# Strassen products in the second MLP projection, with weight sums formed by accumulating transfers

## The chip, the core and the metric

The kernel runs on one core of a Trainium2 chip. Its five engines work side by side: TensorE multiplies matrices into PSUM, VectorE and ScalarE do the elementwise work, GpSimd (POOL) here does masks, a few small operations and some transfers, and SyncE (SP) only issues DMAs. They wait for one another on semaphores. The metric is device time in microseconds (us) of one execution.

## The reference

The program is one layer of a decoder: three mixing branches (a gated delta rule, a gated linear recurrence, attention into a memory), a merge, and then an MLP. The change touches only the MLP, which is, with 256 positions, width 2048 and 8192 hidden columns:

```
h2 = rmsnorm(x, g_pre_mlp[l])
m = jnp.square(jax.nn.relu(h2 @ w_mlp_in[l])) @ w_mlp_out[l]
x = x + rmsnorm(m, g_post_mlp[l])
```

All data are fp32. TensorE's rounded form of fp32 keeps fewer bits, so each operand is split into a high part (its rounded copy) and a low part (the rest), and a product of two operands is taken as three matmuls: high x high, high x low, low x high.

## The kernel before, in words

**Slices.** The hidden columns are cut into 8 slices of 1024 (`NE`, index `e`). `mlp_in(e)` makes the hidden values of slice e, and `mlp_out(e)` multiplies them by the slice's 1024 rows of `w_mlp_out` and adds the result to the accumulators `yacc`. The program goes `mlp_in(0)`, then `mlp_in(e)`, `mlp_out(e-1)` for e = 1 to 7, and `mlp_out(7)` at the end.

**First projection.** `mlp_in(e)` has two units of 512 hidden columns (`unit_stacked`). The weights are the stationary operand there, and the moving one is either 512 wide (high and low activations side by side, a wide matmul) or 256 (high only, a narrow one): 64 wide and 64 narrow matmuls a unit, over 8 weight tiles that are taken in pairs, once with the wide matmuls first and once with the narrow ones. At a unit's end ScalarE copies out one half of each of the four PSUM tiles, VectorE adds the other (four `relu` rows of 128x256), squares the positive part (128x1024), and the value is split into `mh` and `ml`.

**Second projection.** `mlp_out(e)` has four chunks c of 512 output columns; each takes 4 weight tiles of two k-tiles of 128 rows (`KG` = 2), for two token tiles t (`NT` = 2) and three products: 4 x 4 x 2 x 2 x 3 = 192 matmuls of 512 columns. The stationary operands are the tokens, the moving ones the weights. After a chunk VectorE adds two PSUM tiles to `yacc` (in the first slice ScalarE copies them there; in the last one the sums go on to the final norm).

**Weights.** A weight tile is 128 partitions x 2 x 512 fp32, 512 KB. SP's queue loads it (`load_w_raw`) into a ring of raw tiles `w`; `split_w` has ScalarE cast it to `wh` and VectorE subtract to make `wl`, each in a ring of four. A slice takes 16 tiles for each projection. A load can start when the split of the tile that had its buffer is done; a split can write when the matmuls on the old pair are done.

**Order.** The framework's scheduler sets one order of instructions for each engine from a cost model ahead of time, and an engine takes its instructions strictly in that order. Some small jobs are generators in a list `bg`, of which a few steps are pumped after each group of matmuls (`tick`). PSUM has two double tiles in the pool `pmm` and four single tiles in the pool `pbp` (`bank`). All operations of VectorE, ScalarE and TensorE are recorded at one line, L56, the helper that issues them, so that a row is known by its tiles.

Of the kernel before, what the change touches and what calls it, by code (L numbers as in the profile page):

```python
# [10 lines left out]
F32 = mybir.dt.float32  # L11
# [29 lines left out]
def tile_trunk(ctx: ExitStack, tc, a):  # L41
# [31 lines left out]
    wp = ctx.enter_context(tc.tile_pool(name="wp", bufs=4))  # L73
    hp = ctx.enter_context(tc.tile_pool(name="hp", bufs=4))
    gp = ctx.enter_context(tc.tile_pool(name="gp", bufs=25))
    lp = ctx.enter_context(tc.tile_pool(name="lp", bufs=1))
# [4 lines left out]
    pbp = ctx.enter_context(tc.tile_pool(name="pbp", bufs=4, space=bass.MemoryType.PSUM))  # L81

# [24 lines left out]


# [14 lines left out]
    def load_grow(names, c0, q):  # L123
        grow = const(f"grow{c0}", [len(names) * 16, P])
# [84 lines left out]
    def unit(act, nk, src, c0, r0=0, order=None, split=False, post=None, ws=None):  # L209

        if split:
            ps = [bank("mm") for _ in range(2)]
        else:
            both = pmm.tile([P, 1024], F32, tag="mm", name=nm("mm"))
            ps = [both[:, 0:512], both[:, 512:1024]]
        if order is None:
            order = [(g, None) for g in range(nk // KG)]  # L220
        ws = ws or {}
        for i, (g, tt) in enumerate(order):
            k0 = g * KG
            if g not in ws:
                ws[g] = load_w(src, r0 + k0, KG, c0)
            wh, wl = ws[g]
            for j in range(KG):
                kt = k0 + j
                ah, al = act(kt)
                for t in range(NT) if tt is None else (tt,):  # L230
                    o = ps[t]
                    st, sl = ah[:, t * P:(t + 1) * P], al[:, t * P:(t + 1) * P]
                    T.matmul(o, st, wh[:, j, :], start=kt == 0, stop=False)
                    T.matmul(o, st, wl[:, j, :], start=False, stop=False)
                    T.matmul(o, sl, wh[:, j, :], start=False, stop=kt == nk - 1)
            tick()
            if post is not None and i + 1 in post:
                post[i + 1](ps)
        return ps if split else both
# [20 lines left out]
    def unit_stacked(pairs, nk, src, c0, ps):  # L260

        for gg in range(0, nk // KG, 2):
            groups = []
            for g in (gg, gg + 1):
                k0 = g * KG
                groups.append((k0, load_w(src, k0, KG, c0),
                               [flat(pairs[kt // 4][:, kt % 4]) for kt in range(k0, k0 + KG)]))
# [164 lines left out]
    mgt, mlt, caus = const("mgt", [P, P]), const("mlt", [P, P]), const("caus", [P, P])  # L432
    mgtr, onesr = const("mgtr", [P, P], F32R), const("onesr", [P, P], F32R)
    msk2 = const("msk2", [P, 2, P])
    dblk = const("dblk", [P, BL])

    mblk = const("mblk", [P, P])
    rfirst, rsecond = const("rfirst", [P, 1]), const("rsecond", [P, 1])
    mT = {s: const(f"mT{s}", [P, P]) for s in (1, 2, 4, 8, 16, 32, 64)}

    def gen_masks():
# [12 lines left out]
        for s in (1, 2, 4, 8, 16, 32, 64):  # L454
            b = 2 * s
            if b < P:
                cur = cst.tile([P, P], F32, tag=f"blk{b.bit_length() % 2}", name=f"blk{b}")
# [8 lines left out]
            d = cst.tile([P, P], F32, tag="mdiff", name=f"mdiff{s}")  # L466
# [23 lines left out]
    rbm = const("rbm", [P, S])  # L490
# [13 lines left out]
    def gen_start():  # L504
# [11 lines left out]
        crow = const("crow", [96, P])  # L516
        adma(crow, a["conv_a"][0].rearrange("t (c p) -> (t c) p", p=P))
        lrow = const("lrow", [8, P])
# [78 lines left out]
    ccol = const("ccol", [P, 96])  # L597
    lbl1, lba = const("lbl1", [P, 8]), const("lba", [P, 8])
    gna, gnb = const("gna", [P, P]), const("gnb", [P, P])
    alog, dtb = const("alog", [P, 8]), const("dtb", [P, 8])  # L600
# [87 lines left out]
    beta = const("beta", [P, NT, 8])  # L688
    ld = const("ld", [P, NT, 8])
    ldh, ldl = const("ldh", [P, NT, 8], F32R), const("ldl", [P, NT, 8], F32R)  # L690
# [613 lines left out]
    gbc = load_gbc(a["g_post_mix"])  # L1304

# [79 lines left out]
    st2 = const("st2", [P, 8])  # L1385

    def gen_s2():
        for c in range(4):
            for t in range(NT):
                j = g4("junk")  # L1390
                A.activation(j[:, 0:512], xs[c][:, t, :], AF.Square, accum_out=st2[:, t * 4 + c:t * 4 + c + 1])
            yield
# [6 lines left out]

    h2act = act_of(h2T)  # L1400
    yacc = [None] * 4
# [3 lines left out]
    first = [(g, t) for t in range(NT) for g in range(4)] + [(g, None) for g in range(4, 8)]  # L1405

    def gen_turn(r, hi, lo):
# [3 lines left out]
        for hh in range(2):  # L1411
            for q in range(2):
                for t in range(NT):
# [3 lines left out]
            split_psum(pt[:, hh * 512:(hh + 1) * 512].rearrange("p (q s) -> p q s", q=2),  # L1417
                       hi[:, hh * 2:hh * 2 + 2, :], lo[:, hh * 2:hh * 2 + 2, :])
            yield

    def mlp_in(e):
        mt = []
        for u in range(2):
            c0 = e * 1024 + u * 512
            hi, lo = g4("mh", (P, 4, S), F32R), g4("ml", (P, 4, S), F32R)
            r = g4("relu")
            if e == 0 and u == 0:
                ps = unit(h2act, KT, a["w_mlp_in"][0], c0, order=first, ws=ahead)
                A.activation(r, ps, AF.Relu)
                V.scalar_tensor_tensor(out=r, in0=ps, scalar=0.0, in1=r, op0=ALU.max, op1=ALU.mult)  # L1430
                bg.append(gen_turn(r, hi, lo))
            else:
# [7 lines left out]
                unit_stacked(h2B, KT, a["w_mlp_in"][0], c0, ps)  # L1440
                r4 = r.rearrange("p (c s) -> p c s", c=4)
                for c in range(4):
                    A.copy(r4[:, c, :], ps[c][:, S:2 * S])
                    V.tensor_tensor(out=r4[:, c, :], in0=ps[c][:, 0:S], in1=r4[:, c, :], op=ALU.add)
                V.scalar_tensor_tensor(out=r, in0=r, scalar=0.0, in1=r, op0=ALU.max, op1=ALU.mult)
                split_psum(r4, hi, lo)
            mt.append((hi, lo))
        return mt

    def mlp_evac(c, t, p_):  # L1450
        y_ = yacc[c][:, t, :]
        V.tensor_tensor(out=y_, in0=p_, in1=y_, op=ALU.add)
        j = g4("junk")
        A.activation(j[:, 0:512], y_, AF.Square, accum_out=stf[:, t * 4 + c:t * 4 + c + 1])
        return y_

    def final(ps, t):
        y3 = mlp_evac(3, t, ps[t])
        yg = g4("yg")[:, 0:512]
        V.tensor_tensor(out=yg, in0=y3, in1=gb(3), op=ALU.mult)  # L1460
# [4 lines left out]
        for c in range(4):  # L1465
            x_, y_ = xs[c][:, t, :], yacc[c][:, t, :] if c < 3 else yg
# [3 lines left out]
    def mlp_out(e, mt):  # L1470
        for c in range(4):
            args = (act_of(mt), 8, a["w_mlp_out"][0], c * 512, e * 8)
            if e == NE - 1 and c == 3:
# [3 lines left out]
                          post={4: lambda ps: final(ps, 0)})  # L1477
                final(ps, 1)
                continue
            ps = unit(*args, split=c >= 2)  # L1480
            if c < 2:
                ps = [ps[:, t * 512:(t + 1) * 512] for t in range(NT)]
            if e == 0:
                yacc[c] = g4("yacc", (P, NT, 512))
            for t in range(NT):
                if e == 0:
                    A.copy(yacc[c][:, t, :], ps[t])
                elif e < NE - 1:
                    V.tensor_tensor(out=yacc[c][:, t, :], in0=ps[t], in1=yacc[c][:, t, :], op=ALU.add)
                else:  # L1490
                    y_ = mlp_evac(c, t, ps[t])
                    V.tensor_tensor(out=y_, in0=y_, in1=gb(c), op=ALU.mult)

    prev = mlp_in(0)
    bg.append(gen_s2())
    for e in range(1, NE):
        cur = mlp_in(e)
        if e == 4:
            gbc = load_gbc(a["g_post_mlp"])
        mlp_out(e - 1, prev)  # L1500
        prev = cur
    drain()
    mlp_out(NE - 1, prev)
# [14 lines left out]
```

## Time and profile before

| | |
|---|---|
| Runs | 1793.5, 1793.82, 1794.29 us, median 1793.82 |
| The profiled execution, first to last instruction | 1792.7 us, mean granted TensorE clock 0.999 |
| Busy: TensorE | 99%, 9137 matmuls |
| VectorE, ScalarE, POOL | 64%, 51%, 3% |
| DMA | 336.60 MB, 188 GB/s on average |
| Weight tiles of `w_mlp_out` | 128 transfers of 512 KB from SP's queue, 3.9 us from issue to landing |

The median of the runs is 1.1 us above the profiled span. In the profile's rows, "busy" is time in which an instruction of an engine was running; the idle time before an instruction is put down to the semaphore that released it. Buffer numbers are left out of names in the profile, and kept in the rows of the order below.

### The profile page before, as it was taken

The numbers are of one execution on the slowest core, as the hardware profiler recorded it, in microseconds if no ns is written. First come the engines' busy times: TensorE is split into PE (matmuls) and PEld (weight loads), VectorE is DVE, ScalarE is ACT, GpSimd is POOL, SyncE is SP. The second block draws the span as 40 slices with busy tenths as digits, with TensorE's granted clock in tenths as the row PEclk, the third lists the DMA queues.
The fourth block names the chain that finished last, engine by engine and source line by source line (L and its number), as shares of the span: only waits on it lengthen the run. The fifth ranks groups of instructions, "written<-read, shape, count | busy, mean of one in ns | idle before, by whom it ended". The sixth has DMA issues, their size and how long they took to land.

```text
span 1792.7 us, 23771 instructions
## 1 busy us (share of the span) xinstructions
PE 1780.9 (99%) x9137; PEld 1517.3 (85%) x9137; DVE 1151.3 (64%) x1599; ACT 905.8 (51%) x1156; POOL 58.6 (3%) x100
## 2 busy tenths in 40 slices
PE   9999999999999999999999999999999999999998
PEld 7888888888888888888888888888888888888886
DVE  5765768684858488688655557655656565655556
ACT  6644666454554475565444445544444444444433
POOL 0000000400030000000000000000000000000000
PEclk9999999999999999999999999999999999999999
DMA  7665555864587465555566665666666575656554
GB/s 265 209 192 165 172 157 165 226 211 153 157 221 211 122 201 167 165 171 173 168 188 211 214 221 165 188 198 188 192 194 190 188 219 185 196 187 199 187 194 136
DMA packets 176226, 336.60 MB, mean 188 GB/s; under 512 B 13656, under 2 KB 15472, under 8 KB 175728
## 3 DMA queue, kind: packets, MB, share of 16 engines
q1 hardware_dynamic: 169280, 325.10, 58.3%
q0 software_dynamic: 2304, 5.44, 1.6%
q10 hardware_dynamic: 4528, 4.54, 0.9%
q8 instruction: 71, 1.16, 0.3%
q14 instruction: 43, 0.35, 0.1%
HBM read 332.75 MB, written 2.29 MB: 187 GB/s over the span
## 4 chain that ended last, share of the span: by engine, by line
PE 84%; ACT 0%; DVE 0%; issue 0%; DVEq 0%; POOLq 0%; POOL 0%
PE mm L56 80%; PE pa L56 1%; PE kk L56 0%; PE bo L56 0%; PE o L56 0%; PE pzt L56 0%; PE pw L56 0%; PE tr L56 0%; PE y L56 0%; PE oT L56 0%; PE mgT L56 0%; ACT L56 0%; PE dec L56 0%; DVE x L56 0%; ACT bd L56 0%
## 5 line engine op out<-in xcount | busy, mean ns | idle before, releaser
L56 DVE TENSOR_TENSOR wl<-w,wh 128x1024 fp32r<-128x1024 f32 (+1 forms) x610 | 738.4, 1220 | 518.7 <-ACT wh L56 446.9
L56 ACT CAST wh<-w 128x1024 fp32r<-128x1024 f32 (+1 forms) x610 | 636.1, 1049 | 719.2 <-PE mm L56 631.1
L56 PE MATMUL mm<-wh,hh 128*128 128x512 f32 x1152 | 366.3, 392 | 0.0
L56 PEld LDWEIGHTS mm<-wh,hh 128*128 128x128 f32 x1152 | 216.1, 188 | 44.7 <-ACT wh L56 0.3
L56 PE MATMUL mm<-wl,hh 128*128 128x512 f32 x576 | 224.5, 390 | 0.0
L56 PE MATMUL mm<-h2h,wh 128*128 128x512 f32 x960 | 224.4, 390 | 0.0
L56 PEld LDWEIGHTS mm<-h2h,wh 128*128 128x128 f32 x960 | 178.3, 188 | 35.8
L56 PE MATMUL mm<-wh,mh 128*128 128x512 f32 x512 | 199.2, 389 | 0.0
L56 PE MATMUL mm<-wl,mh 128*128 128x512 f32 x512 | 199.2, 389 | 0.0
L56 PE MATMUL mm<-wh,ml 128*128 128x512 f32 x512 | 199.2, 389 | 0.0
L56 PE MATMUL mm<-hh,wh 128*128 128x512 f32 x768 | 185.0, 392 | 0.8 <-ACT z L56 0.8
L56 PEld LDWEIGHTS mm<-hh,wh 128*128 128x128 f32 x768 | 140.9, 188 | 28.5 <-ACT z L56 1.0
L56 PEld LDWEIGHTS mm<-wl,hh 128*128 128x128 f32 x576 | 108.2, 188 | 21.1
L56 PEld LDWEIGHTS mm<-h2h,wl 128*128 128x128 f32 x960 | 119.1, 192 | 2.3
L56 PE MATMUL mm<-h2h,wl 128*128 128x256 f32 x960 | 120.2, 283 | 0.0
L56 PEld LDWEIGHTS mm<-wh,ml 128*128 128x128 f32 x512 | 96.1, 188 | 20.0
L56 PEld LDWEIGHTS mm<-wh,mh 128*128 128x128 f32 x512 | 96.1, 188 | 20.0
L56 PEld LDWEIGHTS mm<-wl,mh 128*128 128x128 f32 x512 | 96.1, 188 | 19.8
L56 PEld LDWEIGHTS mm<-hh,wl 128*128 128x128 f32 x768 | 98.7, 191 | 3.4
L56 PE MATMUL mm<-hh,wl 128*128 128x256 f32 x768 | 101.6, 283 | 0.0
L56 PE MATMUL mm<-wh,oh 128*128 128x512 f32 x128 | 50.1, 392 | 0.0
L56 PE MATMUL mm<-wl,oh 128*128 128x512 f32 x128 | 50.0, 390 | 0.2 <-DVE wl L56 0.2
(339 smaller groups left out, 1770.9 us busy)
## 6 DMA issues: line engine op xcount, KB each, us to landing
w<-in_w_in SPq DMA_DIRECT2D x240, 512.0 KB, 4.3
w<-in_w_mlp_in SPq DMA_DIRECT2D x128, 512.0 KB, 3.8
w<-in_w_mlp_out SPq DMA_DIRECT2D x128, 512.0 KB, 3.9
w<-in_w_out SPq DMA_DIRECT2D x32, 512.0 KB, 4.3
w<-in_w_kv_mem SPq DMA_DIRECT2D x30, 512.0 KB, 5.0
w<-in_w_br_c SPq DMA_DIRECT2D x16, 512.0 KB, 3.9
w<-in_w_br_a SPq DMA_DIRECT2D x16, 512.0 KB, 4.5
w<-in_w_br_b SPq DMA_DIRECT2D x16, 512.0 KB, 3.6
```

The costliest lines, as they stand in the source:

```text
L56: ins = op(*args, **kwargs)
```

## The change

**What it does.** The output columns 0 to 1023 (c = 0 and 1) of slices 0 to 6 are computed by the Winograd form of Strassen's method; the last slice, and the columns from 1024 on, stay as they were. The slice's hidden values are cut into two token halves and two halves of the contraction, its weights into two halves of rows (k1, k2) and of columns: W11, W12, W21, W22, each 512 x 512. Seven products of half size take the place of eight: 7 x 4 k-tiles x 3 = 84 matmuls where there were 96. They are summed over the slices in seven accumulators `acc`, and only in the last slice `joined` combines these into the four blocks of the output, with seven additions of 512 columns on VectorE.

**Weight sums.** Products 6, 4, 5 use sums of weight blocks: W12+W22, W11+W12, W11+W12+W22; product 3 uses that last sum plus W21. The first two are formed in the raw buffers: SP's queue loads W22 and W12, and then a DMA on POOL's queue (`gather`) reads the other summand from DRAM and adds it to what stands in the buffer. The other two are additions of 1024 columns on VectorE (`add_w`). All four are then split as any weight tile. Such a slice takes 22 plain loads of `w_mlp_out` for 16 before (W11, W21 and W22 are loaded for `summed` and again for `bare`), and 4 gathers.

**Activation sums.** `gen_sums`, a background job, makes four sums of the `relu` tiles (128 x 4 x 128) on VectorE and splits two tiles of them; `relu` is kept for it.

**Where it stands.** `seven` gives two functions: `summed` (products 6, 4, 5, 3) and `bare` (products 0, 1, 2), each called for two halves d of the contraction. `summed(0)` comes at the start of the second projection, `summed(1)` in the middle of chunk 2, and `bare` likewise around chunk 3.

**Buffers.** The ring of the MLP's weights is replaced by six raw buffers, `raw0` to `raw5`, and six pairs, `oh0`/`ol0` to `oh5`/`ol5`, taken in turn; the pools of the mixing branches are closed before them to make room. To make room too, x is stored to DRAM (`xd`, four transfers in `gen_s2`) and read back in the last slice (`load_xs`).

```diff
+    def raw(src, k0, c0):
+        w = raws.pop(0)
+        raws.append(w)
+        nc.sync.dma_start(w, src[k0 * P:(k0 + KG) * P, c0:c0 + 512].rearrange("(k p) n -> p k n", p=P))
+        return w
...
+    def gen_sums(rs, ops):
+        yield
+        x1, x2 = rs
+        t0, t1 = slice(0, P), slice(P, S)
+        V.tensor_tensor(out=x1[:, :, t0], in0=x1[:, :, t0], in1=x1[:, :, t1], op=ALU.subtract)
...
+        for x_ in (x1, x2):
+            hi, lo = g4("sh", (P, 4, S), F32R), g4("sl", (P, 4, S), F32R)
+            split_psum(x_, hi, lo)
...
+    def add_w(out, in0, in1):
+        V.tensor_tensor(out=out, in0=in0, in1=in1, op=ALU.add)
+    def gather(w, k0, c0):
+        G.dma_start(w, w_mo[k0 * P:(k0 + KG) * P, c0:c0 + 512].rearrange("(k p) n -> p k n", p=P), accum_op=ALU.add)
...
+        def product(i, w, d):
+            wh, wl = split_w(w, KG, home=operand)
+            for j in range(KG):
+                ah, al = [z[:, d * KG + j, :] for z in acts[i]]
+                begin, end = d == 0 and j == 0, d == 1 and j == KG - 1
+                T.matmul(ps[i], ah, wh[:, j, :], start=begin, stop=False)
+                T.matmul(ps[i], ah, wl[:, j, :], start=False, stop=False)
+                T.matmul(ps[i], al, wh[:, j, :], start=False, stop=end)
+            if d == 1:
+                if e == 0:
+                    A.copy(accs[i], ps[i])
+                else:
+                    V.tensor_tensor(out=accs[i], in0=ps[i], in1=accs[i], op=ALU.add)
+            tick(0.5)
+        def summed(d):
...
+                both = pmm.tile([P, 1024], F32, tag="mm", name=nm("mm"))
+                ps[6], ps[4] = both[:, 0:512], both[:, 512:1024]
+                ps[5], ps[3] = bank("mm"), bank("mm")
+            w12, w22, w11, w21 = raw(w_mo, k1, 512), raw(w_mo, k2, 512), raw(w_mo, k1, 0), raw(w_mo, k2, 0)
+            gather(w22, k1, 512)
+            gather(w12, k1, 0)
+            product(6, w22, d)
+            add_w(w11, w22, w11)
+            product(4, w12, d)
+            add_w(w21, w11, w21)
+            product(5, w11, d)
+            product(3, w21, d)
+        def bare(d):
...
+            product(0, raw(w_mo, k1, 0), d)
+            product(1, raw(w_mo, k2, 0), d)
+            product(2, raw(w_mo, k2, 512), d)
...
+    def load_xs(c):
+        xs[c] = g4("x2", (P, NT, 512))
+        nc.sync.dma_start(xs[c], xd[c])
...
+        for c, part in ((2, summed), (3, bare)):
+            if c == 3 and after is not None:
+                bg.append(after)
+            part(0)
+            ps = unit(act_of(mt), 8, w_mo, c * 512, e * 8, split=True, load=load_in, post={2: lambda ps: part(1)})
```

**What moves in the order.** Four places follow: VectorE around the start of a second projection, before and now; the same place on TensorE; and POOL. The rows are of the third slice; since buffers are taken in turn, other slices have other numbers at the same place. `DMAHW` waits are for transfers of SP's queue, `DMASW` waits for POOL's, `PE`, `Activation` and `DVE` waits for TensorE, ScalarE and VectorE.

VectorE before, from the last weight split of the first projection to the first two sums of the second one (`wl` are weight splits, `relu` and `ml` the end of `mlp_in`'s second unit):

```order
L56 TENSOR_TENSOR relu_2106_12161<-mm_2107_12162,relu_2106_12161 128x256 [waits Activation_49]
L56 TENSOR_TENSOR relu_2106_12161<-mm_2108_12163,relu_2106_12161 128x256 [waits Activation_49]
L56 TENSOR_TENSOR relu_2106_12161<-mm_2109_12164,relu_2106_12161 128x256 [waits Activation_49]
L56 TENSOR_TENSOR relu_2106_12161<-mm_2110_12165,relu_2106_12161 128x256 [waits Activation_49]
L56 TENSOR_TENSOR wl_2149_12415<-w_2147_12412,wh_2148_12414 128x1024 [waits DMAHW7_49,Activation_49]
L56 SCALAR_TENSOR_TENSOR relu_2106_12161<-relu_2106_12161 128x1024 [waits DVE_49]
L56 TENSOR_TENSOR wl_2153_12436<-w_2151_12433,wh_2152_12435 128x1024 [waits DMAHW0_49,Activation_49]
L56 TENSOR_TENSOR ml_2105_12160<-relu_2106_12161,mh_2104_12159 128x1024 [waits Activation_49]
L56 TENSOR_TENSOR wl_2156_12454<-w_2154_12451,wh_2155_12453 128x1024 [waits DMAHW1_49,Activation_49]
L56 TENSOR_TENSOR wl_2159_12472<-w_2157_12469,wh_2158_12471 128x1024 [waits DMAHW2_49,Activation_49]
L56 TENSOR_TENSOR yacc_1802_10358<-mm_2137_12357,yacc_1802_10358 128x512 [waits PE_49]
L56 TENSOR_TENSOR yacc_1802_10358<-mm_2137_12357,yacc_1802_10358 128x512
```

Behind two weight splits each, a sum into `yacc` is the only thing that the second projection asks of VectorE.

VectorE now, from the first sum of weights (`raw0<-raw5`: raw5 holds W12+W22, raw0 holds W11; `raw1<-raw0` is the fourth sum, and `raw4` holds W11+W12) to the second one:

```order
L56 TENSOR_TENSOR raw0_9545<-raw5_1690_9700,raw0_9545 128x1024 [waits DMAHW4_49,DMASW5_49]
L56 TENSOR_TENSOR ol2_9702<-raw2_9697,oh2_9701 128x1024 [waits DMAHW0_49,PE_49,Activation_49]
L56 TENSOR_TENSOR ml_1795_11806<-relu_1796_11807,mh_1794_11805 128x1024 [waits Activation_49]
L56 TENSOR_TENSOR ol3_9704<-raw3_9698,oh3_9703 128x1024 [waits DMAHW1_49,PE_49]
L56 TENSOR_TENSOR raw1_9696<-raw0_9545,raw1_9696 128x1024 [waits DMAHW5_49,DVE_49]
L56 TENSOR_TENSOR ol4_9706<-raw5_1690_9700,oh4_9705 128x1024 [waits Activation_49]
L56 TENSOR_TENSOR ol5_9708<-raw4_9699,oh5_9707 128x1024 [waits DMASW4_49,Activation_49]
L56 TENSOR_TENSOR ol0_9542<-raw0_9545,oh0_9541 128x1024 [waits PE_49,Activation_49]
L56 TENSOR_TENSOR ol1_9544<-raw1_9696,oh1_9543 128x1024 [waits PE_49,Activation_49]
L56 TENSOR_TENSOR raw0_9545<-raw5_1690_9700,raw0_9545 128x1024 [waits DMAHW2_49,DMASW6_49]
```

Both weight sums of half d = 0 are made ahead of the projection's start. The first one is the first row that waits for a gather (`DMASW5`), and `ol4<-raw5`, the split of the gathered tile, is the sixth row from it; the seventh, `ol5<-raw4`, waits for the other gather. The second `raw0<-raw5`, for half d = 1, waits for a gather into the same buffer again. Eight and seven rows above the first one shown stand `ol5<-raw5` and `ol0<-raw0`, the splits of the first projection's tiles that free raw5 for W22's load and raw0 for W11's.

VectorE now, from behind the second `raw0<-raw5` (one `ol2` and four `relu` rows of 128x256 stand between) to the first sum into an accumulator:

```order
L56 TENSOR_TENSOR ol3_9704<-raw3_9698,oh3_9703 128x1024 [waits DMAHW7_49,Activation_49]
L56 SCALAR_TENSOR_TENSOR relu_1801_11975<-relu_1801_11975 128x1024 [waits DVE_49]
L56 TENSOR_TENSOR ol4_9706<-raw5_1690_9700,oh4_9705 128x1024 [waits Activation_49]
L56 TENSOR_TENSOR ol5_9708<-raw4_9699,oh5_9707 128x1024 [waits DMASW7_49,Activation_49]
L56 TENSOR_TENSOR ml_1800_11974<-relu_1801_11975,mh_1799_11973 128x1024 [waits Activation_49]
L56 TENSOR_TENSOR raw1_9696<-raw0_9545,raw1_9696 128x1024 [waits DMAHW3_49]
L56 TENSOR_TENSOR ol0_9542<-raw0_9545,oh0_9541 128x1024 [waits PE_49]
L56 TENSOR_TENSOR ol2_9702<-raw2_9697,oh2_9701 128x1024 [waits DMAHW4_49,Activation_49]
L56 TENSOR_TENSOR ol1_9544<-raw1_9696,oh1_9543 128x1024 [waits Activation_49]
L56 TENSOR_TENSOR ol3_9704<-raw3_9698,oh3_9703 128x1024 [waits DMAHW5_49,Activation_49]
L56 TENSOR_TENSOR acc_1728_10268<-mm_1806_12143,acc_1728_10268 128x512 [waits PE_49]
```

The accumulating row `acc_1728<-mm_1806` of the first PSUM double tile comes behind the splits of half d = 1; before, no row waiting for a gather stood ahead of a sum into `yacc`.

TensorE now, at the middle of chunk 2, in `summed(1)`, half d = 1. The first matmul of the second projection, an `mm_1806<-oh4` of half d = 0, stands 63 rows ahead of the `mm_1806<-oh5` shown:

```order
L56 MATMUL mm_1806_12143<-oh4_9705,sl_1791_11766 128x512
L56 MATMUL mm_1807_12144<-oh0_9541,sh_1792_11784 128x512 [waits Activation_49]
L56 MATMUL mm_1807_12144<-ol0_9542,sh_1792_11784 128x512 [waits DVE_49]
L56 MATMUL mm_1807_12144<-oh0_9541,sl_1793_11785 128x512
L56 MATMUL mm_1807_12144<-oh0_9541,sh_1792_11784 128x512
L56 MATMUL mm_1807_12144<-ol0_9542,sh_1792_11784 128x512
L56 MATMUL mm_1807_12144<-oh0_9541,sl_1793_11785 128x512
L56 MATMUL mm_1808_12145<-oh1_9543,mh_1774_11349 128x512 [waits Activation_49]
L56 MATMUL mm_1808_12145<-ol1_9544,mh_1774_11349 128x512 [waits DVE_49]
L56 MATMUL mm_1808_12145<-oh1_9543,ml_1775_11350 128x512
L56 MATMUL mm_1806_12143<-oh5_9707,sh_1790_11765 128x512 [waits DVE_49]
L56 MATMUL mm_1806_12143<-ol5_9708,sh_1790_11765 128x512
```

`mm_1806` is one PSUM double tile, whose halves are products 6 and 4; the row `mm_1806<-oh5` waits for VectorE, for the sum of the finished half. `mm_1807` and `mm_1808` are products 5 and 3. The matmuls of the four products have gone in among one another, and product 6 ends ahead of product 4, in the other half of the same tile.

POOL now, its gathers at the same border (before, POOL has no instruction at this place):

```order
L1524 DMA raw4_9699<-in_w_mlp_out 128x2x512 [waits DMAHW2_49,DMASW4_49]
L1524 DMA raw5_1690_9700<-in_w_mlp_out 128x2x512 [waits DMAHW3_49,DMASW5_49]
L1524 DMA raw5_1690_9700<-in_w_mlp_out 128x2x512 [waits DMAHW0_49,DMASW6_49]
L1524 DMA raw4_9699<-in_w_mlp_out 128x2x512 [waits DMAHW1_49,DMASW7_49]
```

For each half, W22's buffer (raw5) and W12's (raw4) are gathered into, and each gather waits for its plain load (`DMAHW`). It also waits on one of POOL's own transfers.

More of the change, by code (lines that the diff above doesn't have):

```diff
@@ L1445, in mlp_in @@
                 V.scalar_tensor_tensor(out=r, in0=r, scalar=0.0, in1=r, op0=ALU.max, op1=ALU.mult)
-                split_psum(r4, hi, lo)
+                split_psum(r, hi, lo)
             mt.append((hi, lo))
-        return mt
-    def mlp_evac(c, t, p_):
[L1451 to L1455, printed above, removed]
+            rs.append(r)
```

213 lines of the change are left out of this document (151 added, 62 removed).

## The prediction

> **What bounds the kernel now.** I read the page's table of engines first, then the chain of waits in order of time.
>
> ```profile
> span 1792.7 us, 23771 instructions
> PE 1780.9 (99%) x9137; PEld 1517.3 (85%) x9137; DVE 1151.3 (64%) x1599; ACT 905.8 (51%) x1156; POOL 58.6 (3%) x100
> 1109.31 669.51 PE mm L56 x3391
> 1781.22 4.80 issue
> ```
>
> TensorE is busy throughout, and from 1109 us on, which is nearly the whole MLP, the chain is one unbroken piece of matmuls: nothing else holds it up there. A matmul removed from this piece shortens it, if nothing else becomes late. The share of busy time overstates one matmul, though, since matmuls overlap. What one costs is the step from start to start, read in TensorE's timeline around the border between a slice's first and second projection:
>
> ```profile
> 1154.44 7.44 PE L56 MATMUL mm<-h2h,wh 128*128 128x512 f32 x32
> 1161.72 4.00 PE L56 MATMUL mm<-h2h,wl 128*128 128x256 f32 x32
> 1165.55 3.82 PE L56 MATMUL mm<-h2h,wh 128*128 128x512 f32 x16
> 1169.21 0.39 PE L56 MATMUL mm<-wh,mh 128*128 128x512 f32 x1
> 1169.43 0.39 PE L56 MATMUL mm<-wl,mh 128*128 128x512 f32 x1
> 1169.66 0.39 PE L56 MATMUL mm<-wh,ml 128*128 128x512 f32 x1
> ```
>
> One lasts 0.39 us, but the next starts 0.227 us later; 32 narrow ones take 1165.55 - 1161.72 = 3.83 us, 0.12 us each. The table of windows agrees, cut at this border and at the ends of the projections:
>
> ```profile
> core 0: us, PE busy (x) PEld busy (x) DVE busy (x) ACT busy (x) POOL busy (x), PEclk, DMA share, GB/s
> 1169.20:1212.70 43.50, 43.50 (x193) 36.04 (x192) 23.80 (x23) 21.86 (x26) 0.00 (x0) 1.00 0.62 193
> 1212.70:1257.00 44.30, 44.30 (x257) 39.23 (x256) 22.07 (x22) 19.85 (x25) 0.00 (x0) 1.00 0.61 192
> ```
>
> The second projection of a slice is 192 matmuls in 43.5 us (0.2266 us each), at the full clock (1.00); a first projection takes 44.3 us. VectorE is busy for little more than half of both.
>
> **What is removed.** In each of the first seven slices 84 matmuls take the place of 96: 7 x 12 = 84 fewer, 84 x 0.2267 = **19.0 us** off the unbroken piece. At 0.39 us it would have been 33; that price is wrong because the overlap goes with the matmul. Profile span 1792.7 less 19.0 is 1773.7; the median shown, 1793.82, lies 1.1 above the span, and I add that to every span below.
>
> **What is added, beside TensorE.** These rows carry the prices:
>
> ```profile
> L56 DVE TENSOR_TENSOR wl<-w,wh 128x1024 fp32r<-128x1024 f32 x229 | 278.6, 1224 | 259.1 <-ACT wh L56 213.9 <-PE mm L56 43.4
> L56 ACT CAST wh<-w 128x1024 fp32r<-128x1024 f32 x228 | 240.3, 1054 | 340.1 <-PE mm L56 317.1 <-issue 22.1 <-ACT junk L56 1.0
> L56 DVE TENSOR_TENSOR yacc<-mm,yacc 128x512 f32<-128x512 f32 x56 | 36.1, 685 | 7.4 <-PE mm L56 7.4
> 1338.88 2.36 DVE L56 TENSOR_TENSOR wl<-w,wh 128x1024 fp32r<-128x1024 f32 x2 [2.28 <-PE mm L56]
> 1300.41 1.28 DVE L56 TENSOR_TENSOR yacc<-mm,yacc 128x512 f32<-128x512 f32 x2
> 1325.62 0.75 DVE L56 TENSOR_TENSOR relu<-mm,relu 128x256 f32<-128x256 f32 x2
> w<-in_w_mlp_out SPq DMA_DIRECT2D x128, 512.0 KB, 3.9
> ```
>
> Back to back, VectorE steps 2.36 - 1.22 = 1.14 us for 1024 columns, 0.60 for 512, 0.37 for 256. A second projection now has 22 weight splits (16 before), 4 weight sums, 2 splits of activation sums, and 15 operations of 512 columns: 28 x 1.14 + 15 x 0.60 = 40.9 us of VectorE beside 180 x 0.2267 = 40.8 us of TensorE. VectorE is then as full as TensorE: it hides all of it, but cannot make up a delay within this stretch. In the first projection it has 20 x 1.14 + 8 x 0.37 = 25.8 of 44.3 us, and makes up there. ScalarE: 24 casts x 1.05 = 25.3 us and some copies of 40.8, hidden; with no cover its casts would cost 8 x 1.05 us a slice.
>
> **The one place where a delay reaches TensorE.** Take t = 0 at the first matmul of the second projection (1169.21 above). In the order, TensorE's 64th matmul after t = 0 (`mm_1806<-oh5`) waits for the VectorE row `acc_1728<-mm_1806`. TensorE wants it at 63 x 0.2267 = 14.3 us. VectorE's queue holds, from the second `raw0<-raw5` to that row, 12 operations of 1024 columns, 4 of 256 and the row itself: 12 x 1.14 + 4 x 0.37 + 0.69 = 15.9 us. So that sum must start at S = -1.6, or TensorE waits s = S + 1.6. Queued behind it are the splits that TensorE needs next and the evacuations of its PSUM banks.
>
> When does it start? It needs a plain load of `raw0`, and the second gather into `raw5`. The load: `ol0<-raw0` waits for the last narrow matmul on that operand, 24 narrow and 16 wide ones before t = 0, at -6.5; the matmul's end 0.28, the split 1.22, the load 3.9: S is -1.1 at best, so s is **0.5 us** even with gathers for nothing. The gather's chain, with G0 and G1 for the first and second one from POOL's issue to landing:
>
> 1. `ol5<-raw5` frees the buffer after its last narrow matmul, a whole half projection (64 x 0.347 = 22.2 us) and 16 narrow and 16 wide ones (5.5) before t = 0, at -27.7; + 0.28 + 1.22 + 3.9 for the load and 0.1 for hand-overs: the first gather is issued at -22.2 and lands at -22.2 + G0. The first sum waits for it.
> 2. From there six VectorE rows, in order, to `ol4<-raw5`, which frees the buffer: 5 x 1.14 + 1.22 = 6.9. Load 3.9, hand-overs 0.2, second gather G1.
>
> S = -22.2 + 6.9 + 4.1 + G0 + G1 = G0 + G1 - 11.2, so **s = G0 + G1 - 9.6, never under 0.5**. It holds for six slices. In the first, ScalarE copies stand where VectorE accumulates; there the nearest need is the PSUM bank 2.7 us after t = 0 (`relu` rows, 2 x 1.14 + 0.4 after S), so it waits 1.6 us less.
>
> **The price of a gather**, which no row shows. Bounds are the plain load of the same rows, 3.9 us, and the longest transfer that POOL issued before:
>
> ```profile
> L889 POOL DMA_DIRECT2D lb<-scr x24: 484/487/515, 332.7 to 548.2; - x24
> DMA to landing us min/median/max: 2.9/6.2/9.4
> q1 hardware_dynamic: 169280, 325.10, 58.3%
> ```
>
> At 3.9 each s stays 0.5: 6 x 0.5 = 3.0 us given back. At 9.4 each s = 9.2: 6 x 9.2 + 7.6 = 62.8 us. I take a value near the low end, because a gather moves the weight load's 512 KB in the same rows, where POOL's old transfers had 128 KB for 16 or 32 partitions and were issued in bunches. 325.10 MB in 58.3% of the span is 311 GB/s for full engines, so 1.7 of the 3.9 us is moving bytes. Should the second read of the sum cost nothing, G1 = 3.9; should it double the moving part, 5.6; I take the middle, 4.75. G0 is longer: the partner's gather was issued 1.0 us earlier on the same queue (8 narrow matmuls apart), and with 1.7 to 3.4 us to move it leaves some 1.5: G0 = 6.25. Then s = 1.4 and 6 x 1.4 = **8.4 us** comes back.
>
> A page speaks for the upper of the two prices. The Trainium skill, Collectives: The Full Stack, section "The bandwidth ceiling: the fold count and why AG ≠ RS ≠ AR", holds that an add inside the DMA engines runs at about half a copy's rate, because both operands are read through the same ring; no run here shows it yet. By it the sum would be the first rival's.
>
> **Edits without a price.** Spilling x to DRAM and reading it back is 8 transfers on SP's queue over 600 us; TensorE covers them, and uncovered each is one load's 3.9 us. In the last slice seven VectorE additions (7 x 0.60 = 4.2 us) run beside 43.5 us of matmuls, which do not wait for them. The new weight buffers take over the old ones' space at the MLP's start; the order lets the split of `ol0` stand just ahead of its matmul: 0 to 1.2 us, I take 0. The end after the last matmul is unchanged.
>
> **Sum.** 1792.7 - 19.0 + 8.4 = 1782.1 of span, **1783 us**.
>
> **Rivals.**
>
> *A gather twice a load's work: slower.* G1 = 5.6, and G0 = 5.6 + 3.4 - 1.0 = 8.0: s = 4.0, 6 x 4.0 + 2.4 = 26.4 us against 19.0, time 1801. From s = 3.2, that is G0 + G1 = 12.8, this decides the sign. For it: two reads per byte, and both gathers of a pair in flight with plain loads. Against: the engines are 62% busy in the window.
>
> *The gathers are hidden.* Only the load's 0.5 us is left: 1792.7 - 19.0 + 3.0 + 1.1 = 1778. For it: a plain load's 3.9 us would do. Against: G0 + G1 must stay under 10.1.
>
> *The DMA engines become the bound.* A second projection now takes 26 transfers of 0.524 MB, 13.6 MB in 40.8 us, 334 GB/s against 311: 43.8 us, 3.0 too many. Six buffers hold 10 us of lead, which covers it; if not, 7 x 3.0 = 21 us in place of the 8.4, time 1796.
>
> That the change keeps its matmuls is excluded: the order has 84 wide ones fewer.
>
> **How the numbers follow.** Forecast 0.38 (own range 1778 to 1790, a bit of it reaching no change), hidden gathers 0.12, slow gathers 0.36 (1793 to 1815), DMA bound 0.10, gathers near 9.4 us, time 1838, 0.04. A measurement of this kernel tells about 0.2%, 3.6 us, from no change: 1790.2 to 1797.4. Faster: 0.35 + 0.12 = 0.47. Same: 0.03 of the forecast's, 0.10 of the slow gathers', 0.06 of the DMA's: 0.19. Slower: 0.26 + 0.04 + 0.04 = 0.34. The range 1776 to 1812 holds the forecast, the hidden gathers, the DMA bound and most of the slow ones.
>
> **What would show it.** If right: TensorE's unbroken piece is cut once in each of slices 2 to 7, by 1 to 2 us, with the accumulate of `acc` as releaser; VectorE waits twice a slice for a gather, longer the first time; G0 is over G1, 6 and 5 us. If gathers land under 4.5 us, the cuts shrink to half a microsecond. Cuts of 3 us and more, and gathers of 6 to 8 us, are the slow rival. Cuts spread over the second half of a stretch, released by casts that wait for loads, are the DMA bound. The forecast is wrong altogether if TensorE waits in the first projections too, or if the step of 0.227 us grows.

## The result, and the profile after

The changed kernel takes 1888.38 us (1885.38 to 1888.79, 4 runs) against 1793.79: a ratio of 1.0524, 95% interval 1.0509 to 1.0539. It is 94.6 us slower; the forecast was 1783. The page after, its head and its two weight queues:

```profile
span 1886.4 us, 24013 instructions
PE 1811.8 (96%) x9053; PEld 1509.6 (80%) x9053; DVE 1273.0 (67%) x1736; ACT 959.7 (51%) x1217; POOL 91.7 (5%) x128
PEclk9999999999999999999999999898989998999999
q1 hardware_dynamic: 181856, 351.32, 59.3%
q0 software_dynamic: 9920, 20.13, 6.1%
```

There are 84 matmuls fewer, and yet TensorE is busy 31 us longer; its granted clock has notches in the last third. The table of TensorE's waits has one large entry, seven waits of the same kind:

```profile
PE mm L56 <- DVE relu L56: 61.1, 7, 9.4
PE mm L56 <- DVE ol L56: 2.0, 2, 1.6
```

TensorE's timeline around one of them, at the start of the second slice's second projection (the number in brackets is the idle time and what ended it):

```profile
1291.30 0.40 PE L56 MATMUL mm<-oh,sh 128*128 128x512 f32 x1
1291.53 0.40 PE L56 MATMUL mm<-ol,sh 128*128 128x512 f32 x1
...
1293.83 0.39 PE L56 MATMUL mm<-oh,sl 128*128 128x512 f32 x1
1303.19 0.79 PE L56 MATMUL mm<-oh,sh 128*128 128x512 f32 x1 [8.98 <-DVE relu L56]
1303.78 0.63 PE L56 MATMUL mm<-ol,sh 128*128 128x512 f32 x1
1304.21 0.63 PE L56 MATMUL mm<-oh,sl 128*128 128x512 f32 x1
```

Twelve matmuls run, the thirteenth waits 8.98 us, and the next ones step 0.43 us from start to start (1303.78 to 1304.21) instead of 0.23. The windows before, in and after the slow piece show why:

```profile
core 0: us, PE busy (x) PEld busy (x) DVE busy (x) ACT busy (x) POOL busy (x), PEclk, DMA share, GB/s
1291.30:1303.19 11.89, 2.92 (x13) 2.06 (x11) 2.75 (x4) 2.69 (x5) 2.41 (x2) 0.81 0.88 208
1303.19:1309.01 5.82, 5.82 (x14) 4.56 (x15) 5.82 (x8) 2.91 (x3) 0.00 (x0) 0.50 0.62 193
1309.01:1331.00 21.99, 21.99 (x96) 17.76 (x95) 20.36 (x23) 13.27 (x13) 0.00 (x0) 1.00 0.81 256
```

After the wait the granted clock is 0.50 for 5.8 us; the halved stretch had begun within the wait, where the mean is 0.81. The chain of waits in the same stretch gives the wait's own making:

```profile
1285.90 1.22 DVE ol L56
1287.12 0.02 issue
1287.13 5.62 DMA raw<-in_w_mlp_out
1292.75 0.29 issue
1293.04 7.38 DMA raw<-in_w_mlp_out
1300.42 0.02 issue
...
1301.59 1.22 DVE ol L56
1302.80 0.34 DVE relu L56
```

The split of the first gathered tile frees the buffer (1287.12), a plain load takes 5.62 us, the second gather 7.38, the sum waits for it, and behind the sum on VectorE stand a split and the `relu` row that frees a PSUM tile for TensorE.

There is a second loss, which no table of waits holds. The matmuls of `mm<-wh,h2h` are the first ones of the MLP, so the start of their group is the length of all that the change leaves as it was:

```profile
L56 PE MATMUL mm<-wh,h2h x64: 387/396/503, 1096.7 to 1121.4; 128*128 128x512 f32 x64
```

The same group before:

```profile
L56 PE MATMUL mm<-wh,h2h x64: 387/389/499, 1076.9 to 1101.3; 128*128 128x512 f32 x64
```

The same instructions in the same order took 19.8 us more; ahead of the MLP a 512-wide matmul steps 233.6 ns on the mean, at a granted clock of 1.00, where it stepped 227.5.

The 93.7 us between the spans, worked out from the starts of all matmuls in the two traces (to 0.2 us):

| | us |
|---|---|
| 84 matmuls fewer | -19.0 |
| longer steps before the MLP | +19.8 |
| longer steps in it, at the full clock | +12.1 |
| the seven waits | +61.1 |
| other waits in the MLP | +3.7 |
| steps at half clock (75 of them) | +16.2 |

So three things had to be explained: steps that grew without a wait, waits far over the 1.4 us forecast, and the halved clock behind them.

### The profile page after: what moved, and what is told of

Read it like the earlier page. It is cut to its first block, busy times and chain, and to the rows that moved or that the text cites. A ratio compares the mean times of both kernels' runs of the same rounds, so it can differ in the third digit from the quotient of the medians.

```text
span 1886.4 us, 24013 instructions
## 1 busy us (share of the span) xinstructions
PE 1811.8 (96%) x9053; PEld 1509.6 (80%) x9053; DVE 1273.0 (67%) x1736; ACT 959.7 (51%) x1217; POOL 91.7 (5%) x128
## 3 DMA queue, kind: packets, MB, share of 16 engines
q0 software_dynamic: 9920, 20.13, 6.1%
## 4 chain that ended last, share of the span: by engine, by line
PE 74%; DMA 8%; DVE 2%; issue 1%; ACT 1%; POOL 0%; DVEq 0%; POOLq 0%; ACTq 0%
PE mm L56 70%; DMA raw<-in_w_mlp_out 8%; DVE ol L56 2%; PE pa L56 1%; ACT oh L56 1%; PE kk L56 0%; PE bo L56 0%; PE o L56 0%; DVE ml L56 0%; DVE raw L56 0%; PE pw L56 0%; PE pzt L56 0%; PE tr L56 0%; PE y L56 0%; PE oT L56 0%
## 5 line engine op out<-in xcount | busy, mean ns | idle before, releaser
L56 DVE TENSOR_TENSOR wl<-w,wh 128x1024 fp32r<-128x1024 f32 (+1 forms) x362 | 437.1, 1216 | 254.7 <-ACT wh L56 229.4
L56 ACT CAST wh<-w 128x1024 fp32r<-128x1024 f32 (+1 forms) x362 | 374.4, 1045 | 375.8 <-PE mm L56 320.8
L56 ACT CAST oh<-raw 128x1024 fp32r<-128x1024 f32 x288 | 299.4, 1051 | 374.2 <-PE mm L56 203.1
L56 DVE TENSOR_TENSOR ol<-raw,oh 128x1024 fp32r<-128x1024 f32 x288 | 342.8, 1219 | 110.0 <-ACT oh L56 83.0
L56 PE MATMUL mm<-h2h,oh 128*128 128x512 f32 x960 | 228.9, 394 | 0.0
L56 PE MATMUL mm<-wl,hh 128*128 128x512 f32 x576 | 227.2, 394 | 0.0
L56 PEld LDWEIGHTS mm<-h2h,oh 128*128 128x128 f32 x960 | 178.5, 188 | 39.8
L56 PE MATMUL mm<-oh,mh 128*128 128x512 f32 x372 | 149.8, 403 | 0.0
L56 PE MATMUL mm<-ol,mh 128*128 128x512 f32 x372 | 149.1, 401 | 0.0
L56 PE MATMUL mm<-oh,ml 128*128 128x512 f32 x372 | 148.2, 401 | 0.0
L56 PE MATMUL mm<-h2h,ol 128*128 128x256 f32 x960 | 119.3, 281 | 2.0 <-DVE ol L56 2.0
L56 PE MATMUL mm<-oh,sh 128*128 128x512 f32 x112 | 48.5, 434 | 61.1 <-DVE relu L56 61.1
```

What stands on the lines that cost most here:

```text
L56: ins = op(*args, **kwargs)
```

## Experiments: the longer step

**The first suspect was where the buffers lie.** In the program's placement the change puts the pool of weight buffers on the other side of SBUF, counted from its upper end. They start 32 bytes off a multiple of 64 there, while the operands of the large matmuls were at one place within 512 bytes before. `shifted` puts the weight buffers of the kernel before 32 bytes off in this way:

```diff
+    edge = ctx.enter_context(tc.tile_pool(name="edge", bufs=1))
+    edge.tile([P, 8], F32, tag="edge", name="edge")
     wp = ctx.enter_context(tc.tile_pool(name="wp", bufs=4))
+    edge2 = ctx.enter_context(tc.tile_pool(name="edge2", bufs=1))
+    edge2.tile([P, 8], F32, tag="edge2", name="edge2")
     hp = ctx.enter_context(tc.tile_pool(name="hp", bufs=4))
```

> The kernel before with its weight buffers moved 32 bytes, all else at its old alignment and in its old order. Theory (start address): the MLP starts about 20 us later, 512-wide matmuls step 231 to 238 ns instead of 227, and the whole is 25 to 38 us longer, 1819 to 1832. Rival (address plays no part): 1794.

`shifted` took 1826.03 us (ratio 1.0178, 1.0161 to 1.0195). The same group in its trace:

```profile
L56 PE MATMUL mm<-wh,h2h x64: 387/396/501, 1094.9 to 1119.7; 128*128 128x512 f32 x64
```

Eighteen us late at the MLP, with no instruction changed, added or moved: so the address makes the steps longer. `aligned` mends the changed kernel by the same 32 bytes:

```diff
+    edge = ctx.enter_context(tc.tile_pool(name="edge", bufs=1, side="right"))
+    edge.tile([P, 8], F32, tag="edge", name="edge")
     wp = weights.enter_context(tc.tile_pool(name="wp", bufs=4, side="right"))
```

> The changed kernel with one unused tile of 32 bytes a partition ahead of the weight buffers on their side of SBUF, so that every weight buffer starts at a multiple of 64 bytes as before the change, not 32 bytes off it; every engine's order is the same. Theory (start address): the first part of the program, which the change leaves alone, took 1096.7 us instead of 1076.9 up to the MLP because operands start 32 bytes off; it returns to about 1077, the wide matmuls step 227 ns again in the MLP too, and the time falls by 19.8 us and 10 to 16 more, to about 1855. The gathers, the stall of 8 to 9 us a slice and the halved clock behind it stay. Rival (the longer step has another cause, the chip or the longer program): 1888, unchanged.

`aligned` took 1867.19 us (1.0411, 1.0395 to 1.0426): 21 us better, not 33, and the MLP starts at 1083.1, not 1077. Wide steps are 230.2 ns on the mean. The multiple of 64 was not the whole rule. In this kernel the weights stand 64 bytes from the other operands within 128, in the kernel before at 0. `together` (one pool of 32 bytes ahead of everything, in the kernel before) and `aligned96` (24 instead of 8 floats in the diff above) ask whether each address counts or the distance.

> The kernel before with everything in SBUF moved by 32 bytes, so that both operands of every matmul stand 32 bytes off a multiple of 64, at the same distance from one another as before. Theory (what counts is how the two operands stand to each other): no change, 1794. Rival (what counts is each address by itself): as in the shifted kernel, 1826.

> The changed kernel with a gap of 96 bytes instead of 32 ahead of the weight buffers: they stand at the same place within 1024 bytes as the other operands, as before the change. In the aligned kernel (32 bytes) they stood 64 bytes apart from them, and the MLP still started at 1083.1 us against 1076.9. Theory (the two operands' distance): the MLP starts at 1077, wide matmuls step 227 ns, and the time falls by another 10 to 14 us to about 1855. Rival (a multiple of 64 is all that counts, the rest has another cause): 1867 as in the aligned kernel.

`together` took 1794.07 us (1.0000, 0.9991 to 1.0010): no change. `aligned96` took 1858.13 (1.0357, 1.0339 to 1.0374), with the MLP's start at 1076.0 and wide steps of 227.3. So the distance counts, not each address. `apart128` (32 floats behind the weight pool of the kernel before) tests how far the block reaches:

> The kernel before with 128 bytes between the weight buffers and all that lies behind them, so that a matmul's two operands stand 128 bytes apart within 1024, where they stood at 0. The runs so far have 0 (227 ns a wide step), 32 and 96 (233), 64 (230). Theory (only the place within 128 bytes counts): 1794. Rival (the place within a larger block counts): 1800 to 1826.

`apart128` took 1825.42 us (1.0176, 1.0159 to 1.0193): the rival was right, 128 bytes apart is as bad as 32. Grouped by how far the next matmul's stationary tile starts from this one's moving operand, the steps of these traces come out so:

| distance within 512 bytes | mean step of a wide matmul, ns |
|---|---|
| 0, in the kernels that have no other distance | 227.2 to 227.4 |
| 0, among other distances (the changed kernel, `aligned`) | 229.1 and 229.3 |
| 32 (either way) | 233.1 to 233.5 |
| 64 | 229.5 one way, 233.3 the other |
| 96 | 233.4 to 234.3 |
| 128 | 232.3 to 232.9 |

So the changed kernel lost 1888.4 - 1858.1 = 30 us to 96 bytes. The second row says that the distance of one pair is not the whole account of its step. And in nearly all of these pairs the matmul's own stationary tile stands at the same distance as the next one's, so which of the two counts is open. What in the chip makes it so, no run shows.

## Experiments: the wait for the gathers

**What in the gather is slow?** `plain` makes the 28 gathers plain transfers of the same rows on the same queue, in the `aligned` kernel (the two sums are then missing from the result):

```diff
-        G.dma_start(w, w_mo[...].rearrange("(k p) n -> p k n", p=P), accum_op=ALU.add)
+        G.dma_start(w, w_mo[...].rearrange("(k p) n -> p k n", p=P))
```

> As the aligned kernel, but the 28 transfers of POOL's queue are plain loads that replace what stands in the buffer; the sums W12+W22 and W11+W12 are left out, so the result differs, and order and waits are the same. Theory (the add inside the transfer costs the time): the transfer lands in 4 to 5 us instead of 7.5, the stall falls from 9 to 3 or 4 us a slice, the clock is not halved behind it, and the time is about 1800. Rival (POOL's queue costs it, its 1.2 us for an issue and the crowd of loads): the transfers still take 7 us and more, and the time stays within 10 us of the aligned kernel.

`plain` took 1834.35 us (1.0223, 1.0208 to 1.0238), 33 us under `aligned`. The rows of the gathers, after and in `plain`:

```profile
L1524 POOL DMA_DIRECT2D raw<-in_w_mlp_out x28: 1194/1203/1284, 1168.0 to 1784.3; - x28
...
DMA to landing us min/median/max: 6.2/7.5/11.8
```

```profile
L1526 POOL DMA_DIRECT2D raw<-in_w_mlp_out x28: 722/722/781, 1154.4 to 1730.0; - x28
...
DMA to landing us min/median/max: 4.3/5.4/8.1
```

And POOL's queue in the pages of `plain` and of the kernel before (packets, MB, their time as a share of 16 engines' span):

```profile
q0 software_dynamic: 6336, 20.13, 3.9%
```

```profile
q0 software_dynamic: 2304, 5.44, 1.6%
```

Without the add, POOL issues in 0.72 instead of 1.20 us, and the transfer lands in 5.4 instead of 7.5. The seven waits fall from 9.1 us each in `aligned` to 3.9:

```profile
PE mm L56 <- DVE relu L56: 27.4, 7, 6.5
```

Landing and waits came out near the expectation, the time 34 us above its 1800: `aligned` itself was 12 us above the 1855 that this was reckoned from, and the clock is still halved behind six of the seven waits.

These shares tell what moving the bytes takes: 1.6% of 1792.7 us before is 28.7 us of all engines, 6.1% of 1886.4 after is 115.1, so a gather takes (115.1 - 28.7) / 28 = 3.1 us; in `plain`, 3.9% of 1832.2, it is 1.5. An add doubles the moving part. The packets tell how: the rows of q0 give (9920 - 2304) / 28 = 272 packets a gather and (6336 - 2304) / 28 = 144 a plain transfer, and in the traces the former are of 2 KB and the latter of 4 KB, at 193 ns each (a few packets of 4 bytes aside). The Trainium skill's rule in Collectives: The Full Stack, "The bandwidth ceiling: the fold count and why AG ≠ RS ≠ AR", stated there for a reduction over a ring of cores, is about half a copy's rate for an add in the DMA engines; the rate here agrees with that, while two reads per byte, the page's reason, were not seen as such. Beside this moving part, 4.4 us of the 7.5 are left with the add, and 3.9 of the 5.4 without; what fills them was not followed. The wait of 3.9 us a slice that stays in `plain` goes with the second trip itself, a load and then another transfer: `vsums`, next, has no such trip, and no such wait.

**Without the second trip.** `vsums` has VectorE make the two sums from tiles that are loaded anyway; `vsums96` is the same with the gap of 96 bytes:

```diff
-            gather(w22, k1, 512)
-            gather(w12, k1, 0)
+            add_w(w22, w12, w22)
+            add_w(w12, w11, w12)
             product(6, w22, d)
```

> As the aligned kernel, but the two sums that the gathers form are made by VectorE from the raw tiles that are loaded anyway: 4 more additions of 1024 columns a slice, no gather. Theory (the gathers make the stall): TensorE waits under 2 us a slice, the clock is never halved, and the time is 1776 to 1790, faster than before the change. Rival (VectorE becomes the bound, 45.5 us of work beside 40.8 of TensorE): TensorE waits about 4 us a slice, 7 x 4.6 = 32 us over 1775, about 1807.

> As vsums (all four weight sums on VectorE, no gather), with the gap of 96 bytes. Theory (its TensorE waited 1.6 us in the whole MLP, so what kept it at 1793 was the longer step): 1793 less 6 before the MLP and 7 to 9 in it, 1778 to 1780, and the whole saving of 19.0 us less some 3 us of waits shows. Rival (VectorE's fuller queue costs something that the gaps don't show): 1787 or more.

`vsums` took 1792.99 us (0.9993, 0.9984 to 1.0003). TensorE waits 1.6 us in the whole MLP, as expected, and the time is above the expected 1776 to 1790 because the operands still stood 64 bytes apart. `vsums96` took **1782.2** us (0.9933, 0.9919 to 0.9948), less than both kernels and 2 us above its expectation of 1778 to 1780. Its page and TensorE's waits:

```profile
span 1780.5 us, 23962 instructions
PE 1765.2 (99%) x9053; PEld 1499.1 (84%) x9053; DVE 1302.3 (73%) x1764; ACT 961.5 (54%) x1217; POOL 57.9 (3%) x100
```

```profile
PE mm L56 <- DVE ol L56: 2.4, 5, 0.8
```

From the MLP's first to its last matmul it takes 694.2 us, where the kernel before took 706.9: 12.7 of the 19.0 us are there, and the rest went into short waits, the longest 0.8 us: those of the table, and about 0.1 us each in some thirty steps that have no entry there. VectorE carries 28 more additions than in the changed kernel (1764 to 1736 instructions), and is not the bound.

**One gather, and a longer lead.** `one96` keeps the gather for W11+W12 alone; `seven96` keeps both, adds a buffer (as `vsums7` does to `vsums96`) and loads W22 ahead of W12:

```diff
-            gather(w22, k1, 512)
+            add_w(w22, w12, w22)
             gather(w12, k1, 0)
```

```diff
-    raws = [at(wx, "raw0", F32)]
+    raws = [at(wx, "raw0", F32), at(wx, "raw6", F32)]
...
-            w12, w22, w11, w21 = raw(w_mo, k1, 512), raw(w_mo, k2, 512), raw(w_mo, k1, 0), raw(w_mo, k2, 0)
+            w22, w12, w11, w21 = raw(w_mo, k2, 512), raw(w_mo, k1, 512), raw(w_mo, k1, 0), raw(w_mo, k2, 0)
```

> As aligned96, with the gather for W11+W12 kept and W12+W22 made by VectorE: 2 gathers a slice, and 2 more additions of 1024 columns. The gather now waits for that addition, and only the split of its own tile waits for it. Theory (a chain with one gather after the other sets the stall): one gather of about 7 us in each half, not in a crowd, leaves the first sums free; TensorE waits 1 to 5 us a slice, time 1790 to 1815. Rival (any gather on VectorE's queue costs its 7.5 us): a stall of 8 us, about 1850.

> As aligned96, with gathers, but with a seventh raw buffer, and W22 loaded ahead of W12: in the order, the buffer of the first gather comes free two weight tiles of the first projection earlier (2.8 us each), and that of the second one no longer waits for the split of the first gathered tile. Theory (the stall is the chain from free buffer to load, gather, sum, six rows, load, gather, sum): the first gather is issued some 5 us earlier, the second sum starts about 1 us after the projection's start instead of 9, TensorE waits 2 to 4 us a slice, and the time is about 1800. Rival (the gathers are short of transfer rate, not of time ahead): the stall stays over 6 us and the time over 1835.

> As vsums96 (all sums on VectorE) with the seventh raw buffer. Theory (what is left of TensorE's waits there, some 6 us in the MLP, most of them a few tenths behind weight splits, comes from loads that are just late): 1777 to 1780. Rival (VectorE itself is late, a buffer more does not help): 1782, unchanged.

`one96` took 1788.05 us (0.9970, 0.9960 to 0.9981), a little better than expected: its 14 gathers still take 6.3 us, but nothing on the path waits for them long. TensorE's waits there:

```profile
PE mm L56 <- DVE acc L56: 5.0, 6, 1.0
```

`seven96` took 1846.1 us (1.0282, 1.0258 to 1.0306), 46 us over its expectation; its trace is of its fastest execution, 1837.5. The seven waits fell from 63.0 us in `aligned96` to 33.2, 4.7 each and not 2 to 4. The gathers grew slower (median 9.0 us, for 7.8 in `aligned96`), and the second pair is issued 16 to 18 us behind the first, for 22 to 24; whether the one makes the other, no run shows. And the new ring brought a wait of its own in the first slice:

```profile
PE mm L56 <- DVE relu L56: 33.2, 7, 6.2
PE mm L56 <- ACT oh L56: 9.9, 1, 9.9
```

`vsums7` has the same 9.9 us once, and that is why it takes 1793.19 (0.9998, 0.9988 to 1.0007) and not 1777 to 1780; its other waits in the MLP, 4.0 us, are not under the 2.5 of `vsums96`. In its trace the cast that TensorE waits for starts on ScalarE at 1134.35, behind six squares of x (`junk<-x`, a part of `gen_s2`) that take from 1130.66 on; in `vsums96` two casts, at 1128.05 and 1129.87, stand ahead of these squares. So at least a part of the 9.9 us is another order on ScalarE, which came with the larger ring, and not the ring's loads.

## An experiment: the halved clock

`fill96` gives TensorE 36 matmuls by a tile of zeros six matmuls ahead of the place where it would wait, in the `aligned96` kernel:

```diff
+            if i == 6 and d == 0:
+                for n in range(36):
+                    T.matmul(ps[6], zr, wh[:, n % KG, :], start=False, stop=False)
```

> As aligned96, with 36 matmuls by a tile of zeros into product 6's PSUM at the place where TensorE waits in each of the seven slices (36 x 0.227 = 8.2 us, in a stall of 8 to 10.6). They add nothing to the result; VectorE's order around them changes a little. Theory (the wait itself makes the chip halve TensorE's clock for about 10 us, of which some 5 fall on matmuls and cost half): the clock stays full, and 7 x 2.4 = 17 us go, to about 1838. Rival (the halved clock comes from something else, or the matmuls only come on top): 1855 or more.

`fill96` took 1853.4 us (1.0330, 1.0315 to 1.0345): the clock is full, but only 4.7 us are gone, not 17. Its mean granted clock is 0.999, that of `aligned96` 0.981. Its waits:

```profile
PE mm L56 <- DVE acc L56: 8.3, 6, 1.4
PE mm L56 <- DVE relu L56: 3.2, 5, 1.1
```

The matmuls of zeros take 7 x 36 x 0.227 = 57 us, and the waits left are 15.4 us, 73 together; in `aligned96` the waits were 66.1 (all counted from start to start of the matmuls, which adds 0.1 to 0.2 us to each wait of the table). So 15.3 us of slow steps went, 6.5 us of waits came, and 3.6 in steps that are a little longer, whose cause is open. The new waits are the six for `acc`: at full speed TensorE gets there before VectorE's sum is done, and waits 1.3 to 1.4 us, which the slow clock had hidden. That the wait causes the halved clock is shown; that some 6.5 of the 15.3 us had been cover for VectorE's lateness is what the account of the waits says. The Trainium skill, TensorE: Matmul & The Clock Gate, "What's actually happening", gives windows of about 3.4 us after which an idle TensorE falls to half its clock; the traces agree: the halved stretches behind the seven waits of the changed kernel are 10.2 or 6.8 us long, and in `plain`, where the waits are 2.9 to 4.1 us after the first slice, 3.4 or 6.8, with none behind one wait of 3.2.

## Why the prediction was wrong

**The matmuls removed.** Right. Taking waits and slow steps out of the MLP of `aligned96` leaves 687 us, against 706 before: 19.

**The one place where a delay reaches TensorE.** The mechanism was right and the place half right. The waits come once a slice, from the second sum of weights, through the chain that was written out; they end at the thirteenth matmul, at the PSUM tile that `relu` frees, in all seven slices. The six VectorE rows between the two sums took what was forecast, 6.9 us: the first sum starts as below, and the chain above has the buffer free at 1287.12.

```profile
1280.20 1.23 DVE L56 TENSOR_TENSOR raw<-raw,raw 128x1024 f32<-128x1024 f32 x1 [6.66 <-DMA raw<-in_w_mlp_out]
```

The prediction had the thirteenth matmul for the first slice alone and put the others at the 64th matmul. With a late sum the nearer need decides; the other one shows in `fill96` and `one96`, where `acc` is the releaser, in `fill96` with 1.3 to 1.4 us, near the 1.6 that the forecast put between the two needs. VectorE waits twice a slice for a gather, as foretold, but not longer the first time: 6.66 us, then 9.93, in the second slice.

**The price of a gather.** This is the step that failed first. I took G0 = 6.25 and G1 = 4.75 us, near the low end; the first gathers into W22's buffer took 10.6 on the mean of the seven slices, the second ones 7.0. The wait was 61.1 / 7 = 8.7 us a slice, for 1.4. The formula s = G0 + G1 - 9.6 gives 8.0 with these prices, but that is near for the wrong need, the 64th matmul. At the thirteenth the rows behind the sum take as long as the twelve matmuls ahead, so that the wait is nearly S, the sum's own start: S = 10.6 + 7.0 - 11.2 = 6.4 by the chain as written, 8.9 as measured. The first gather is issued 21.4 us ahead of the projection and not 22.2, and from the first sum to the second gather's issue it is 12.7 us and not 11.0. In `plain` the two gathers take 6.6 and 5.7, S would be 1.1, and is 4.1. The reasoning for the low end ("POOL's old transfers had 128 KB for 16 or 32 partitions and were issued in bunches") set aside the one row of POOL's queue in favour of a row of another queue, and even without the add this queue took 5.4 us, where the forecast had 3.9 as the least and SP's loads beside it took 5.1. The bound kept for it, 9.4 each, 62.8 us in all, was nearest to the truth, and I gave it a chance of 0.04.

**The plain loads' price.** A load of `w_mlp_out` took 3.9 us before and 5.2 after, as medians; the one on the chain took 5.1 on the mean of the slices (5.62 in the chain above), 1.2 of the 1.7 us by which 12.7 is over 11.0. I took the price from a kernel with 16 of these loads a slice, and the change makes it 22 and 4 gathers. In `vsums96`, with 22 and no gather, it is still 4.8, so the gathers are not the main cause.

**Edits without a price.** "The new weight buffers take over the old ones' space at the MLP's start": this failed outright. The edit also moves `wp`, the pool of the weights ahead of the MLP, to the other side, and the move of the pools cost 30 us. The order was unchanged by it, and I priced it by that alone; the prediction named the sign of it ("if the step of 0.227 us grows") without a case for it.

**What a wait brings after it.** The sum had no term for the clock. It cost 16.2 us of slow steps; filling the waits gave back 5.

**The rivals.** A gather twice a load's work: its moving part was twice, as that rival said, but at 1801 it had the rest of the landing at a load's price. The DMA engines as the bound: not seen, since 61 of 65 us of waits end on the gathers' chain and none stands in a projection's second half. By the sum as it stood, with the measured gathers and nothing else (6 x 8.0 + 6.4 in place of 8.4), the time would have been 1829; of the other 59 us, 30 are addresses and 16 the slow clock, and most of the rest is waits, 64.8 us for the 54.4 of that sum.

## What to carry to other kernels

Price a transfer from the row of the queue that will issue it, and count a buffer that is filled by two transfers in turn as two trips on the path; a sum that VectorE has room for was cheaper here than the DMA that spares it. When a change moves pools, compare where moving and stationary operands start within 512 bytes, before and after: it costs nothing to mend with a few bytes of padding, and no table of waits shows it. First compare how long the untouched part of the program took.

## What was not expected of the hardware

- A 512-wide fp32 matmul steps 227 ns in the kernels here whose moving operands and stationary tiles all start at the same place within 512 bytes, and 229 to 234 ns at the distances tried (32, 64, 96, 128 bytes); over this program 1.8% at 32 and at 128, with all else the same.
- An accumulating transfer of 512 KB takes POOL 1.20 us to issue, 3.1 us of all DMA engines' time and 7.5 us to land, a plain one on the same queue 0.72, 1.5 and 5.4.
- In the changed kernel waits of 8 to 9 us halved TensorE's clock for 6.8 or 10.2 us each time, and yet, in `aligned96`, keeping it full was worth only 4.7 us of seven such waits.
